# A two-layer attention trunk in split float32: side work moved off the key copies, gate products between transposes, value products in one batch, a merge ordered by branch

## The chip, the core and the metric

The kernel runs on one core of a Trainium2 chip. The engines are named as in the profile: PE is TensorE (matrix products), PEld its weight loads, DVE is VectorE, ACT is ScalarE, POOL is GpSimd and SP is SyncE, which issues the weight DMAs. The metric is the device time of one execution in microseconds (us); smaller is better.

## What is computed

A trunk of two layers over 256 context tokens and 256 latent tokens of width 1024. Cut to what matters here:

```python
for l in range(2):
    shift, scale, gate, shift2, scale2, gate2 = split(silu(c) @ w_ada[l] + b_ada[l])  # adaLN
    h = modulate(rms_norm(x), shift, scale)
    p = h @ w_in[l]                          # gate logits | c_q | c_kv | k_rope | na q,k,v
    mq = rms_norm(c_q) @ w_uq;  mk, mv = rms_norm(c_kv) @ w_ukv
    y_mla = softmax(norm(mq) @ norm(mk).T) @ mv              # 8 heads, all keys
    y_na = softmax([window scores + bias, context scores]) @ nv   # 8 heads
    g = sigmoid(gate logits)
    x = x + gate * ((g_a * (y_mla @ w_mla_o) + g_b * (y_na @ w_na_o)) @ w_out)
    x = x + gate2 * (relu(modulate(rms_norm(x), shift2, scale2) @ w_ff1) ** 2 @ w_ff2)
return x_latent
```

Context tokens attend to context tokens alone. In the second layer only latent tokens go on behind the keys and values, so its query side is 256 tokens wide instead of 512.

## The kernel before

All is float32, and every product is made of three passes on PE over operands split into a high and a low part (`mm3`, lines 99 to 103: high by high, low by high, high by low). A weight block of 0.5 MB is loaded raw on SP's queue, ACT makes its high part (L129), DVE the low part (L130); three split blocks can be held, five raw ones. PSUM is split into banks A (two), B (three), C (two) and D (one). In the first layer a product streams 512 columns, in the second 256.

Order of the stages in a layer: projections of `c_q`, `c_kv` and rope keys; queries (`w_uq`) and keys and values (`w_ukv`, copied out of PSUM at L738 by DVE and L739 by ACT, statistics at L604 and L605); six of the 16 gate blocks (`gates`, 24 PE products a block); latent attention (MLA), neighbourhood projections (`chunk_na`, keys, queries, values, 192 products of 256 columns each, with head norms on POOL at L608, L179 and L978), neighbourhood attention (NA), the rest of the gates, the merge (lines 1031 to 1060), the output projection and the feed-forward part. The tile scheduler writes the order of each engine from priorities: what `high_priority` marks goes first when ready, and products of later stages are put where nothing else was ready.

In an attention stage heads go in pairs. `prep_mla` and `prep_na` transpose queries and keys on PE into a bank C (lines 781, 786, 800, 805) and split them; scores go to banks B; `soft` makes the probabilities; `flip` transposes them (L872) and ACT (L876) and DVE (L878) copy them out; `mix` makes the value products (L892), in one batch for the context queries (four instructions) and one for the latent queries (eight).

The adaLN vectors of later use are side work on DVE: `ada_side`, with a product of a weight row by a scalar (L250), sums of further rows (L254), a transpose and a reduction (L265, L266) and a small PE product (L272). It is a generator, which `step(n)` advances by n parts; `step` is called once for every second key copy, once behind each block of `proj_a`, four times at the end of a feed-forward block, and `step(99)` ends it before a stage needs it. The lines of the key copy that the change touches:

```python
                if hf == 1 and tk % 2:
                    k_stat(tk - 1)
                if tk % 2:
                    step()
```

The merge, for each of eight column blocks j, makes the product of branch a (`ym`) and of branch b, then scales both by the gates (L1048), adds them (L1052) and splits the sum (L1053, L1054); the low part of the latent attention's output, `y1l`, is made by DVE at L1018 ahead of it.

Of the kernel before, what the change touches and what calls it, by code (L numbers as in the profile page):

```python
# [45 lines left out]
def trunk(ctx: ExitStack, tc, t):  # L46
# [77 lines left out]
    split = []  # L124

# [338 lines left out]
    for l in range(DEPTH):  # L464
# [218 lines left out]
        def gates(n, bank="A"):  # L683
            for _ in range(n):
                f = ngate[0]
                proj_a(w_in, 0, KD, f, 1, (H, Lo), c_q, lambda _, o: gate_evac(f, o), bank)
                ngate[0] += 1

# [43 lines left out]
        for hf in range(2):  # L732
            def evac(tk, o):
                hs = slice(hf * 4, (hf + 1) * 4)
                src = o.rearrange("p (h d) -> p h d", h=4)
                rs = rk[:, tk:tk + 1]
                dst = mk[:, tk, hs, 0:NOPE]
                nc.vector.tensor_copy(dst, src[:, :, 0:NOPE])  # L738
                nc.scalar.activation(out=mv[:, tk, hs, :], in_=src[:, :, NOPE:128], func=AF.Copy, scale=rs)  # L739
                head_ss(krr[:, tk, hs], dst, 4, NOPE, rs)  # L740
                if hf == 1 and tk % 2:
                    k_stat(tk - 1)
                if tk % 2:
                    step()
# [16 lines left out]
        gates(NG0[l], "B")  # L761
# [16 lines left out]
        def prep_mla(h):  # L778
            o = ps("C")
            for tk in range(q0, 4):  # L780
                nc.tensor.transpose(o[:QK, tk * 128:(tk + 1) * 128], mq[:, tk, h, :], ident)
# [3 lines left out]
            for tk in range(4):  # L785
                nc.tensor.transpose(o[:QK, tk * 128:(tk + 1) * 128], mk[:, tk, h, :], ident)
# [9 lines left out]
        def prep_na(hp):  # L796
            cs = slice(2 * hp * HD, (2 * hp + 2) * HD)
            o = ps("C")
            for tk in range(q0, 4):
                nc.tensor.transpose(o[:, tk * 128:(tk + 1) * 128], nqk[:, tk, cs], rev if tk >= 2 else ident)  # L800
# [3 lines left out]
            for tk in range(4):  # L804
                nc.tensor.transpose(o[:, tk * 128:(tk + 1) * 128], nqk[:, 4 + tk, cs], ident)
# [60 lines left out]
        def flip(P, K, perm):  # L866
            out = []
            for kp in range(K // 256):
# [5 lines left out]
                pT_ = ap.tile([128, 2, 256], F32, tag="PT", name="PT", bufs=4)  # L874
# [9 lines left out]
        def mix(yo, st, K, vsel, hp, ta, tb):  # L884

            oc = slice(st * 256, (st + 1) * 256)
            nkt = K // 128
            for kt in reversed(range(nkt)):
                for z, tr in ((1, tb), (0, ta)):
                    lead = z == 1 and kt == nkt - 1  # L890
                    with nullcontext() if lead else tc.high_priority(2000):
                        mm = nc.tensor.matmul(  # L892
                            yo[z * 64:(z + 1) * 64, oc], vsel(kt, 2 * hp + z), tr[kt // 2][:, kt % 2, :],
                            start=kt == nkt - 1, stop=kt == 0, tile_position=(0, z * 64))
                    if not lead:
                        tc.keep_in_program_order(mm)

        def attend_mla(vsel, ev):
            nxt = prep_mla(0)
            for hp in range(NH // 2):  # L900
                pa = nxt
                pb = prep_mla(2 * hp + 1)
                yo = ps("D")
                for gi, (toks, K, st) in enumerate(groups):
# [4 lines left out]
                    mix(yo, st, K, vsel, hp, ta, tb)  # L909
                ev(hp, yo[:, c_q])  # L910

        def attend_na(vsel, ev):

            nxt = prep_na(0)
            for hp in range(NH // 2):
# [13 lines left out]

                for gi, (toks, K, st) in enumerate(groups):  # L930
# [18 lines left out]
                    mix(yo, st, K, vsel, hp, ta, tb)  # L949
# [57 lines left out]
        gates(16 - ngate[0])  # L1007
# [24 lines left out]
        for f in range(0, 8, 2):  # L1032
# [4 lines left out]
            for j in range(2):  # L1037
                zs = [None, None]
                fs = slice(j * 128, (j + 1) * 128)
                g2 = g2f[:, :, j]  # L1040
                for b in (0, 1):
                    (h, lo), (yh, yl) = wab[b], ys[b]
# [3 lines left out]
                    zs[b] = o  # L1046
                for b in range(2):
                    nc.vector.scalar_tensor_tensor(out=g2[:, b], in0=g2[:, b], scalar=1.0, in1=zs[b],  # L1048
                                                   op0=ALU.add, op1=ALU.mult)
                eng = nc.vector if f + j >= 6 else nc.gpsimd  # L1050
                m = sp.tile([128, TT], F32, tag="tmp", name="m", bufs=NTMP)
                eng.tensor_tensor(out=m[:, :TQ], in0=g2[:, 0], in1=g2[:, 1], op=ALU.add)  # L1052
# [133 lines left out]
        def ff2(g, a):  # L1186
# [13 lines left out]
            step(4)  # L1200
# [53 lines left out]
        step(99)  # L1254
        pre_ctx = po_ctx
# [55 lines left out]
```

## Time and profile before

| | us |
|---|---|
| runs | 1308.4, 1308.9, 1310.21 |
| median | 1308.9 |
| profiled execution | 1308.73 |
| its span in the profile | 1306.9 |
| PE busy in the span | 1272.0 |
| DVE busy | 907.8 |
| ACT busy | 582.3 |
| POOL busy | 262.3 |

The span runs from the first to the last recorded instruction; the execution's own time is 1.8 us longer. In the first layer, by the trace: key projection to 125, gates to 157.6, MLA from its first score at 163.9 to its last value product at 237.3, neighbourhood projections to 282.3, NA to 352.2, the rest of the gates to 379.2. The hand-over to the second layer lies at 834 to 846, the second layer's merge at 1062 to 1077. A row of a timeline gives start, duration, engine, line, operation, output and inputs with their shapes, and in brackets the idle time in front with the instruction that ended it. PE's products overlap, so what a product costs is read from one start to the next, not from its duration.

### The profile page before, as it was taken

What the parts mean: (1) busy time and instruction counts of PE and PEld (TensorE: products, weight loads), DVE (VectorE), ACT (ScalarE), POOL (GpSimd) and SP (SyncE); (2) the same over time, 40 slices, a digit from 0 to 9 for tenths busy, and PEclk for the clock granted to TensorE, in tenths of its full rate; (3) what the DMA queues carried; (4) which work ended last, traced back from release to release, by engine and by line L of the source; (5) the groups of instructions that cost most, each with busy time, mean ns of one, the idle gap of its engine ahead of it and who ended that gap; (6) DMA issues with size and microseconds to landing.
All of it is one profiled execution on the core that took longest, in us unless ns stands there. A gap on an engine that the chain in (4) does not pass through costs nothing.

```text
span 1306.9 us, 20364 instructions
## 1 busy us (share of the span) xinstructions
PE 1272.0 (97%) x7831; PEld 1093.3 (84%) x7831; DVE 907.8 (69%) x1547; ACT 582.3 (45%) x1054; POOL 262.3 (20%) x258
## 2 busy tenths in 40 slices
PE   7998999999999999999999999899999999999997
PEld 5697888986787898888888888899889779999896
DVE  4559687688985579899675675766763967665553
ACT  4455277445523344422322312366664645554452
POOL 0317402411004003210201200019132111121011
PEclk9998999999999999999999999899999999999999
DMA  9855600364486326566566574387214657646652
GB/s 292 291 110 161 209 29 22 100 193 64 110 308 202 99 64 197 163 204 200 167 197 209 170 226 141 115 172 213 74 44 119 129 179 206 169 160 192 193 186 89
DMA packets 241857, 208.01 MB, mean 159 GB/s; under 512 B 24464, under 2 KB 220816, under 8 KB 241376
## 3 DMA queue, kind: packets, MB, share of 16 engines
q1 hardware_dynamic: 231728, 190.16, 50.6%
q10 hardware_dynamic: 9520, 16.29, 3.5%
q8 instruction: 61, 1.00, 0.3%
q0 software_dynamic: 512, 0.27, 0.1%
q14 instruction: 36, 0.29, 0.1%
HBM read 195.15 MB, written 11.53 MB: 158 GB/s over the span
## 4 chain that ended last, share of the span: by engine, by line
PE 55%; DVE 2%; POOL 2%; issue 2%; ACT 1%; DMA 0%; POOLq 0%; ACTq 0%; DVEq 0%
PE psB L101 7%; PE psB L103 7%; PE psB L102 7%; PE psA L101 6%; PE psA L103 6%; PE psA L102 6%; PE psC L103 4%; PE psC L101 4%; PE psC L102 4%; DVE wlo L130 1%; PE psC L872 1%; PE psD L892 1%; ACT whi L129 1%; PE psB L926 1%; PE psD L101 0%
## 5 line engine op out<-in xcount | busy, mean ns | idle before, releaser
L130 DVE TENSOR_TENSOR wlo<-raw,whi 128x1024 fp32r<-128x1024 f32 (+3 forms) x252 | 310.6, 1234 | 189.8 <-ACT whi L129 188.6
L129 ACT ACTIVATE whi<-raw 128x1024 fp32r<-128x1024 f32 (+3 forms) x252 | 260.5, 1035 | 351.3 <-PE psB L102 116.7
L254 DVE SCALAR_TENSOR_TENSOR ada<-raw,silu,ada 128x1024 f32<-128x1024 f32 (+1 forms) x126 | 156.3, 1272 | 0.2
L102 PE MATMUL psA<-wlo,h 128*128 128x256 f32 (+2 forms) x408 | 120.9, 296 | 2.4 <-DVE wlo L130 2.4
L101 PE MATMUL psA<-whi,h 128*128 128x256 f32 (+2 forms) x408 | 121.0, 297 | 1.1 <-ACT h L344 1.1
L103 PE MATMUL psA<-whi,h 128*128 128x256 f32 (+2 forms) x408 | 120.8, 296 | 0.0
L101 PE MATMUL psB<-h,whi 128*128 128x256 f32 (+1 forms) x272 | 91.8, 338 | 0.1
L102 PE MATMUL psB<-h,whi 128*128 128x256 f32 (+1 forms) x272 | 91.8, 338 | 0.0
L103 PE MATMUL psB<-h,wlo 128*128 128x256 f32 (+1 forms) x272 | 91.6, 337 | 0.0
L101 PE MATMUL psA<-h,whi 128*128 128x512 f32 (+1 forms) x248 | 87.6, 354 | 1.1 <-ACT h L344 1.0
L102 PE MATMUL psA<-h,whi 128*128 128x512 f32 (+1 forms) x248 | 87.3, 352 | 0.2 <-DVE h L346 0.2
L103 PE MATMUL psA<-h,wlo 128*128 128x512 f32 (+1 forms) x248 | 87.1, 351 | 0.0
L102 PEld LDWEIGHTS psA<-wlo,h 128*128 128x128 f32 x408 | 78.3, 192 | 4.7 <-DVE wlo L130 2.6
L101 PEld LDWEIGHTS psA<-whi,h 128*128 128x128 f32 x408 | 78.3, 192 | 3.3 <-ACT h L344 1.6
L103 PEld LDWEIGHTS psA<-whi,h 128*128 128x128 f32 x408 | 78.3, 192 | 2.3 <-issue 0.4
L1165 POOL TENSOR_TENSOR h<-s,h 128x512 fp32r<-128x512 f32 (+1 forms) x32 | 38.0, 1190 | 168.5 <-ACT h L1164 151.1
L1165 POOL TENSOR_TENSOR fl<-s,fa 128x512 fp32r<-128x512 f32 (+1 forms) x32 | 35.3, 1104 | 164.8 <-ACT fa L1164 164.8
L101 PE MATMUL psB<-G,whi 128*128 128x512 f32 (+2 forms) x192 | 66.8, 348 | 0.0
L103 PE MATMUL psB<-G,wlo 128*128 128x512 f32 (+2 forms) x192 | 66.3, 345 | 0.3 <-DVE wlo L130 0.3
L102 PE MATMUL psB<-G,whi 128*128 128x512 f32 (+2 forms) x192 | 66.5, 346 | 0.0
L101 PE MATMUL psC<-G,whi 128*128 128x258 f32 (+2 forms) x200 | 62.6, 313 | 0.0
L103 PE MATMUL psC<-G,wlo 128*128 128x258 f32 (+2 forms) x200 | 62.5, 312 | 0.0
(388 smaller groups left out, 3333.0 us busy)
## 6 DMA issues: line engine op xcount, KB each, us to landing
raw<-in_w_ff_dram SPq DMA_DIRECT2D x128, 512.0 KB, 4.3
raw<-in_w_ada_dram SPq DMA_DIRECT2D x80, 512.0 KB, 3.7
raw<-in_w_in_dram SPq DMA_DIRECT2D x62, 512.0 KB, 4.6
raw<-in_w_out_dram SPq DMA_DIRECT2D x16, 512.0 KB, 4.6
spare<-in_w_ada_dram SPq DMA_DIRECT2D x12, 512.0 KB, 8.9
xT_d<-xT SPq DMA_DIRECT2D x2, 2048.0 KB, 13.1
bias<-in_rpb_dram SPq DMA_DIRECT2D x64, 64.0 KB, 7.1
g_d<-g ACTq DMA_DIRECT2D x16, 256.0 KB, 3.9
```

Of the source, the lines that this page charges most:

```text
L101: nc.tensor.matmul(out, sh, mh, start=first, stop=False)
L102: nc.tensor.matmul(out, sh, ml, start=False, stop=False)
L103: nc.tensor.matmul(out, sl, mh, start=False, stop=last)
L129: nc.scalar.activation(out=hi, in_=src, func=AF.Copy)
L130: split[:] = [nc.vector.tensor_tensor(out=lo, in0=src, in1=hi.bitcast(F32), op=ALU.subtract).ins]
L254: nc.vector.scalar_tensor_tensor(out=a, in0=raw[:, c:c + w], scalar=sc, in1=a, op0=ALU.mult, op1=ALU.add)
L872: nc.tensor.transpose(o[:, kt * 256 + i * 128:kt * 256 + (i + 1) * 128], pt[:, (kp * 2 + kt) * 128:(kp * 2 + kt + 1) * 128], perm if K == ...
L892: mm = nc.tensor.matmul(yo[z * 64:(z + 1) * 64, oc], vsel(kt, 2 * hp + z), tr[kt // 2][:, kt % 2, :], start=kt == nkt - 1, stop=kt == 0, t ...
L926: mm = nc.tensor.matmul(os[z], q_[zs, cs], k_[zs, :K], start=n == 0, stop=n == 2)
L1165: nc.gpsimd.tensor_tensor(out=al[:, f, :], in0=s[:, :TQ], in1=ah[:, f, :].bitcast(F32), op=ALU.subtract)
```

## The change

Five edits. (1) The key copies no longer call `step`. (2) `pace`: behind the first `ff2` block of the first layer each block of `proj_a` calls `step(2)`, until the layer ends; the `step(4)` per `ff2` block is gone. (3) The gate blocks become a generator that yields one PE product at a time; in the first layer `chain` puts one of them, in fixed order, behind each transpose of queries and keys. In the second layer `chain` only raises the priority of the transposes behind the first. (4) `mix` takes both query groups of a pair, so their value products form one batch, the latent group first; the flipped probabilities of the context group get two tiles of their own (`PTc`). In the second layer there is one group, and its batch is as before. (5) The merge goes by branches: a for both column blocks of a pair, then b for both, each product scaled right away.

```diff
+    pace = [1]
...
                 evac(f + j, o)
                 flush()
-                step()
+                step(pace[0])
...
+        def gate_mms(bank):
+            while ngate[0] < 16:
                 f = ngate[0]
-                proj_a(w_in, 0, KD, f, 1, (H, Lo), c_q, lambda _, o: gate_evac(f, o), bank)
                 ngate[0] += 1
+                h, lo = wsplit(wraw(w_in, 0, KD, f * 128, 128), KD, 128)
+                o = ps(bank[0])[:, :TQ]
+                for k in range(KD):
+                    for n, (a, b) in enumerate(((h, H), (h, Lo), (lo, H))):
+                        yield nc.tensor.matmul(o, a[:, k], b(k)[:, c_q], start=k == n == 0, stop=k == KD - 1 and n == 2)
+                gate_evac(f, o)
+                flush()
+                step(pace[0])
+                yield None
...
+        def chain(trs):
+            for i, tr in enumerate(trs):
+                with nullcontext() if i == 0 else tc.high_priority(2000):
+                    mm = tr()
+                if l:
+                    continue
+                if i:
+                    tc.keep_in_program_order(mm)
+                with tc.high_priority(2000):
+                    g = next(gstream, None)
+                    if g is None:
+                        g = next(gstream, None)
+                if g is not None:
+                    tc.keep_in_program_order(g)
...
-                if tk % 2:
-                    step()
...
-            for tk in range(4):
-                nc.tensor.transpose(o[:QK, tk * 128:(tk + 1) * 128], mk[:, tk, h, :], ident)
+            chain([lambda tk=tk: nc.tensor.transpose(o[:QK, tk * 128:(tk + 1) * 128], mk[:, tk, h, :], ident)
+                   for tk in range(4)])
...
-                    mix(yo, st, K, vsel, hp, ta, tb)
+                    parts.append((st, K, ta, tb))
+                mix(yo, vsel, hp, parts)
...
-            for j in range(2):
-                zs = [None, None]
...
+            for b in (0, 1):
+                (h, lo), (yh, yl) = wab[b], ys[b]
+                for j in range(2):
...
-            step(4)
+            pace[0] = 2
```

DVE at the first key copies, before; `mqk` is the tile of queries and keys, `qrs` and `krr` the statistics, `ada` the side work:

```order
L130 TENSOR_TENSOR wlo<-raw,whi 128x1024
L254 SCALAR_TENSOR_TENSOR ada<-raw,silu,ada 128x512 x6
L605 TENSOR_REDUCE qrs<-sq 128x2
L254 SCALAR_TENSOR_TENSOR ada<-raw,silu,ada 128x512 x2
L605 TENSOR_REDUCE qrs<-sq 128x2
L130 TENSOR_TENSOR wlo<-raw,whi 128x1024
L738 COPY mqk<-psB 128x4x64 x2
```

and with the change:

```order
L131 TENSOR_TENSOR wlo<-raw,whi 128x1024
L606 TENSOR_REDUCE qrs<-sq 128x2
L131 TENSOR_TENSOR wlo<-raw,whi 128x1024
L606 TENSOR_REDUCE qrs<-sq 128x2
L774 COPY mqk<-psB 128x4x64 x2
L251 TENSOR_SCALAR ada<-raw,silu 128x512 x2
L606 TENSOR_REDUCE krr<-sq 128x4
L251 TENSOR_SCALAR ada<-raw,silu 128x512
```

All of the side work that stood ahead of the copies (two groups are shown) stands behind the first of them now, from its first product of a row and a scalar on.

PE at the end of a pair of the MLA stage (the third), before; the operands are `qk` for scores, `P` probabilities, `whi,h` a neighbourhood projection product, and `mv` values:

```order
L872 MATMUL psC<-ident,P 128x128 x4
L103 MATMUL psA<-whi,h 128x256
L872 MATMUL psC<-ident,P 128x128 x4
L102 MATMUL psB<-qk 128x256
L781 MATMUL psC<-ident,mqk 96x128 x4
L103 MATMUL psB<-qk 128x256
L102 MATMUL psB<-qk 128x256
L103 MATMUL psB<-qk 128x256
L892 MATMUL psD<-PT,mv 64x256 x8
L786 MATMUL psC<-ident,mqk 96x128 x4
L101 MATMUL psA<-whi,h 128x256
```

and with the change, at the end of the first pair (here `h,whi` is a gate product):

```order
L693 MATMUL psA<-h,whi 128x512
L815 MATMUL psC<-ident,mqk 96x128
L693 MATMUL psA<-h,wlo 128x512
L815 MATMUL psC<-ident,mqk 96x128
L693 MATMUL psA<-h,whi 128x512
L932 MATMUL psD<-PT,mv 64x256 x8
L932 MATMUL psD<-PTc,mv 64x256 x4
L820 MATMUL psC<-ident,mqk 96x128
L693 MATMUL psA<-h,whi 128x512
L820 MATMUL psC<-ident,mqk 96x128
```

The neighbourhood projection's products have left this place, each transpose of queries or keys is followed by a gate product, and the value products of both groups stand together. In the whole stage, from the first score to the last value product, 193 projection products become 48, and 48 gate products are added (16 more stand in front of it). Behind the stage 343 projection products become 528.

PE at the end of the neighbourhood projections, before, with the first pair's transposes behind the last value projection (`nqk` is the tile of queries and keys, `whi_3115` a block of the value projection):

```order
L102 MATMUL psA_3170<-wlo_3116,h_207 128x256
L103 MATMUL psA_3170<-whi_3115,h_208 128x256
L800 MATMUL psC_3231<-ident_70,nqk_2446 128x128 x2
L800 MATMUL psC_3231<-rev_72,nqk_2446 128x128 x2
L805 MATMUL psC_3240<-ident_70,nqk_2446 128x128 x4
L101 MATMUL psA_3977<-h_207,whi_3973 128x512
L102 MATMUL psA_3977<-h_208,whi_3973 128x512
```

and with the change, some 180 products earlier (`whi_3078` and `whi_3084` are the value projection's first blocks):

```order
L103 MATMUL psA_3088<-whi_3078,h_208 128x256
L834 MATMUL psC_3322<-rev_72,nqk_2537 128x128
L693 MATMUL psA_2263<-h_207,whi_2259 128x512
L101 MATMUL psA_3088<-whi_3084,h_207 128x256
L834 MATMUL psC_3322<-rev_72,nqk_2537 128x128
L693 MATMUL psA_2263<-h_208,whi_2259 128x512
L693 MATMUL psA_2263<-h_207,wlo_2260 128x512
L839 MATMUL psC_3335<-ident_70,nqk_2537 128x128
L693 MATMUL psA_2263<-h_207,whi_2259 128x512
```

The first two query transposes (L834) stand directly behind the query projection now, 12 products of the value projection come between them and the other two, of which the first row shows the last, 179 come later, and gate products stand between. Of the gates 81 products are left behind the last value product of NA instead of 118, and ahead of the second L272 product and of `y1l` PE has six merge products instead of 17.

## Rows read from the trace of the kernel before

**Rows 1.** Page, busy time of the engines over the span (us, share, instructions)

```profile
PE 1272.0 (97%) x7831; PEld 1093.3 (84%) x7831; DVE 907.8 (69%) x1547; ACT 582.3 (45%) x1054; POOL 262.3 (20%) x258
```

**Rows 2.** Table of windows: busy us (records) of each engine, granted clock, DMA

```profile
117.00:125.00 8.00, 7.23 (x22) 5.72 (x23) 8.00 (x16) 5.84 (x13) 7.68 (x9) 0.65 0.42 124
125.00:157.60 32.60, 32.60 (x145) 27.00 (x144) 25.56 (x32) 10.45 (x16) 21.69 (x19) 1.00 0.72 218
...
163.90:237.30 73.40, 72.36 (x535) 60.59 (x533) 57.53 (x163) 49.84 (x117) 12.79 (x12) 1.00 0.10 30
237.30:282.30 45.00, 45.00 (x367) 44.24 (x365) 29.88 (x33) 19.20 (x36) 14.96 (x12) 1.00 0.55 161
282.30:352.20 69.90, 68.95 (x425) 46.93 (x424) 62.62 (x151) 40.79 (x99) 6.38 (x5) 1.00 0.42 82
352.20:379.20 27.00, 27.00 (x121) 22.30 (x120) 25.25 (x24) 6.86 (x10) 0.00 (x0) 1.00 0.82 264
...
834.00:846.00 12.00, 7.95 (x41) 7.20 (x40) 9.27 (x25) 2.38 (x6) 0.70 (x1) 0.73 0.54 160
1062.00:1077.00 15.00, 12.69 (x98) 11.84 (x98) 7.24 (x15) 4.44 (x8) 5.10 (x6) 1.00 0.73 226
```

**Rows 3.** Timeline of PE at the first keys: start, us, line, [idle <-releaser]

```profile
112.45 0.39 PE L103 MATMUL psB<-whi,G 128*128 128x512 f32 x1
117.77 0.79 PE L101 MATMUL psB<-whi,G 128*128 128x512 f32 x1 [4.93 <-ACT mv L739]
```

**Rows 4.** Timeline of VectorE ahead of the key copies

```profile
108.91 4.06 DVE L254 SCALAR_TENSOR_TENSOR ada<-raw,silu,ada 128x512 f32<-128x512 f32 x6
...
113.15 2.26 DVE L254 SCALAR_TENSOR_TENSOR ada<-raw,silu,ada 128x512 f32<-128x512 f32 x2
```

**Rows 5.** Timeline of ScalarE, copy of the first values

```profile
117.24 0.47 ACT L739 ACTIVATE mv<-psB,rk 128x256 f32<-128x256 f32 x1 [7.47 <-DVE mqk L738]
```

**Rows 6.** Timeline of PE, last vector product and single and grouped transposes

```profile
160.96 0.33 PE L272 MATMUL psC<-red,m 128*128 128x64 f32 x2
161.12 0.60 PE L781 MATMUL psC<-ident,mqk 128*96 128x128 f32 x4
...
161.68 0.28 PE L103 MATMUL psA<-whi,h 128*128 128x256 f32 x1
...
202.76 0.28 PE L103 MATMUL psA<-whi,h 128*128 128x256 f32 x1
202.89 0.27 PE L872 MATMUL psC<-ident,P 128*128 128x128 f32 x1
...
203.11 0.28 PE L102 MATMUL psA<-wlo,h 128*128 128x256 f32 x1
```

**Rows 7.** Groups of PE by shape in 163.9 to 237.3 us (busy, mean ns)

```profile
L102 PE MATMUL psA<-wlo,h 128*128 128x256 f32 x65 | 19.0, 292 | 0.0
```

**Rows 8.** Timeline of ScalarE, last copy of the neighbourhood queries

```profile
255.72 0.66 ACT L973 ACTIVATE nqk<-psA 128x256 f32<-128x256 f32 x2 [0.38 <-PE psA L103]
```

**Rows 9.** Timeline of GpSimd, norm of the last query tokens

```profile
264.29 0.20 POOL L608 TENSOR_SCALAR nrs<-nrs 128x8 f32<-128x8 f32 x1
...
266.28 1.04 POOL L978 TENSOR_TENSOR nqk<-nqk,nrs 128x512 f32<-128x512 f32 x1
```

**Rows 10.** Timeline of VectorE from the last probabilities to the merge

```profile
346.50 0.48 DVE L842 TENSOR_SCALAR P<-P,ri 128x512 f32<-128x512 f32 x1
...
365.05 9.65 DVE L254 SCALAR_TENSOR_TENSOR ada<-raw,silu,ada 128x1024 f32<-128x1024 f32 x8
...
383.43 0.68 DVE L1018 TENSOR_TENSOR y1l<-yv,ym 128x512 fp32r<-128x512 f32 x1
```

**Rows 11.** Timeline of PE between the layers

```profile
836.92 0.40 PE L102 MATMUL psA<-wlo,h 128*128 128x288 f32 x1 [2.37 <-DVE wlo L130]
...
839.74 1.23 PE L330 MATMUL psC<-ident,rt 128*128 128x128 f32 x4 [0.56 <-POOL rt L179]
842.07 0.61 PE L101 MATMUL psA<-whi,h 128*128 128x288 f32 x1 [1.11 <-ACT h L344]
```

More of the change, by code (lines that the diff above doesn't have):

```diff
@@ L681, in trunk, with gates @@
         ngate = [0]
-        def gates(n, bank="A"):
-            for _ in range(n):
+        def gate_mms(bank):
+            while ngate[0] < 16:
                 f = ngate[0]
-                proj_a(w_in, 0, KD, f, 1, (H, Lo), c_q, lambda _, o: gate_evac(f, o), bank)
                 ngate[0] += 1
+                h, lo = wsplit(wraw(w_in, 0, KD, f * 128, 128), KD, 128)
[7 more added lines that the diff above has]
+                yield None
+        gbank = ["B"]
+        gstream = gate_mms(gbank)
+        def gates(n):
+            while n and ngate[0] <= 16:
+                mm = next(gstream, 0)
+                if mm == 0:
+                    return
+                n -= mm is None
+        def chain(trs):
[12 more added lines that the diff above has]
+                    tc.keep_in_program_order(g)
         if l == 0:
@@ L759, in trunk @@
             q_end = q_fin(tk)
-        gates(NG0[l], "B")
+        gates(NG0[l])
+        gbank[0] = "A"
         step(99)
@@ L779, in prep_mla @@
             o = ps("C")
-            for tk in range(q0, 4):
-                nc.tensor.transpose(o[:QK, tk * 128:(tk + 1) * 128], mq[:, tk, h, :], ident)
+            chain([lambda tk=tk: nc.tensor.transpose(o[:QK, tk * 128:(tk + 1) * 128], mq[:, tk, h, :], ident)
+                   for tk in range(q0, 4)])
             qh, ql = qk_tile(TQ), qk_tile(TQ)
@@ L798, in prep_na @@
             o = ps("C")
-            for tk in range(q0, 4):
-                nc.tensor.transpose(o[:, tk * 128:(tk + 1) * 128], nqk[:, tk, cs], rev if tk >= 2 else ident)
+            chain([lambda tk=tk: nc.tensor.transpose(o[:, tk * 128:(tk + 1) * 128], nqk[:, tk, cs],
+                                                     rev if tk >= 2 else ident) for tk in range(q0, 4)])
             qh, ql = qk_tile(TQ), qk_tile(TQ)
@@ L803, in prep_na @@
             o = ps("C")
-            for tk in range(4):
-                nc.tensor.transpose(o[:, tk * 128:(tk + 1) * 128], nqk[:, 4 + tk, cs], ident)
+            chain([lambda tk=tk: nc.tensor.transpose(o[:, tk * 128:(tk + 1) * 128], nqk[:, 4 + tk, cs], ident)
+                   for tk in range(4)])
             kh, kl = qk_tile(), qk_tile()
@@ L882, in trunk, with mix @@
         groups = ([] if last else [([0, 1], LC, 0)]) + [([2, 3], TT, 1)]
[L884 to L896, printed above, removed]
+        def mix(yo, vsel, hp, parts):
+            lead = True
+            for st, K, ta, tb in reversed(parts):
+                oc = slice(st * 256, (st + 1) * 256)
+                nkt = K // 128
+                for kt in reversed(range(nkt)):
+                    for z, tr in ((1, tb), (0, ta)):
+                        with nullcontext() if lead else tc.high_priority(2000):
+                            mm = nc.tensor.matmul(
+                                yo[z * 64:(z + 1) * 64, oc], vsel(kt, 2 * hp + z), tr[kt // 2][:, kt % 2, :],
+                                start=kt == nkt - 1, stop=kt == 0, tile_position=(0, z * 64))
+                        if not lead:
+                            tc.keep_in_program_order(mm)
+                        lead = False
         def attend_mla(vsel, ev):
@@ L948, in attend_na @@
                     ta, tb = (flip(p, K, rev) for p in P)
[L949 removed]
+                    parts.append((st, K, ta, tb))
+                mix(yo, vsel, hp, parts)
                 ev(hp, yo[:, c_q])
@@ L1005, in trunk @@
         attend_na(lambda kt, h: nv[:, kt, h * HD:(h + 1) * HD], ev_y2)
-        gates(16 - ngate[0])
+        gates(16)
         step(99)
@@ L1254, in trunk @@
         step(99)
+        pace[0] = 1
         pre_ctx = po_ctx
```

21 lines of the change are left out of this document (12 added, 9 removed).

## Prediction

> **What bounds the kernel now.** I read the page first. PE is busy 97% of the span, VectorE 69% and ScalarE 45% [rows 1], so time can be won at PE's few waits and clock dips, or by giving PE fewer products; and it is lost wherever PE's queue, which takes its instructions in order, meets a result that is not there. Next came the table of windows by stage [rows 2]. In the four attention stages of the first layer, 163.9 to 379.2 us, PE stands idle for about two microseconds in all. That is no proof that PE sets the length there: products that nothing waits for (the neighbourhood projection in the first stage, the gates later) are put into its gaps. In 163.9 to 237.3 us there are 193 such projection products (three lines, 65 of one of them in [rows 7]). At 0.12 us each, the slot that [rows 6] shows for one, they are 23 of PE's 72 us there. What is left, 49 us, is less than VectorE's 57.5 [rows 2]. So the stage is a chain through PE, ScalarE and VectorE, whose gaps are filled. The question for this change is where it takes the filling from.
>
> **Sum against the profiled execution**, 1308.7 us (span 1306.9), within 0.2 us of the median 1308.9.
>
> *Keys: -7.3.* The second bank of key products waits 4.93 us for a ScalarE copy [rows 3], which itself sat behind VectorE's first copy for 7.47 us [rows 5]. Ahead of that VectorE copy stand eight adaLN sums, six of which take 4.06 us [rows 4]. The change moves all of them behind the copies, so the wait goes whole, 4.9 to 5.1 us. After the wait the clock is 0.65 over the window 117 to 125: 22 products take 7.2 us, where the next window has 32.6 us for 145, or 0.225 each [rows 2]; 22 of those are 4.9 us, so 2.3 come back too. Nothing hides this gain, since PE is full behind it.
>
> *From the gates to the first score: +3.2.* The adaLN sums have not gone; 16 more of VectorE's short ones now lie between the key copies and the adaLN product in front of the first transposes, at 4.06/6 = 0.68 us each 10.8 us. Before, PE reached that product at 160.96 [rows 6] after filling its wait with 28 projection products (3.4 us); in the new order no product stands there. With no idle VectorE would be done just as PE is done with the gates (wait 0); with as much idle as before, 13 us late. I take 4, nearer to the lower end, since the gap that is seen there is 3.4. Gates 32.6, wait 4, and 16 transposes each with its gate product: a transpose costs 0.11 whether four stand together (161.12 to 161.68, less one product of 0.12) or one stands between products (202.76 to 203.11 less two products) [rows 6]. So 16 x 0.336 = 5.4, together 42.1 against 38.9 (125.0 to 163.9).
>
> *Transposes apart: 0.* By the same rows nothing is won by parting them: 0.11 each way. The Trainium skill's page "TensorE: Matmul & The Clock Gate", in its part on what happens when a matmul is issued, says that the next weights can be loaded during the running matmul, and gives 0.056 us from start to start at 128 columns; by that, a transpose behind a long product would cost half, and the 96 parted ones of this layer would give an estimated 5 us of PE time. The trace does not agree: 0.11 in both settings.
>
> *Latent attention, 73.4 us: 0.* In the new order 48 projection products are left there, 145 fewer (-17.4 us of PE work), with 48 gate products added (0.225 each, +10.8) and value batches joined (four fewer entries and exits at 0.2, -0.8). PE's work falls to about 65 us. Bounds: -8.7, if the stage is as short as that work; +7, if two of a pair's four groups of transposes lie on the chain, since four now take 1.35 us instead of 0.44. I take the length as it was, because the projection products that filled it held up nothing that a chain waits for.
>
> *Projection behind it, 45.0 us: +21.3.* The 145 products, with the 40 that used to fill the wait for the adaLN product and the first transposes, stand here now: 343 become 528. 185 x 0.12 = 22.2, less four gate products 0.9. This stage is PE alone (45.00 of 45.00 busy, [rows 2]), so nothing hides it.
>
> *A new wait in it: +5.4.* The query transposes now come straight behind the query projection, with 12 products between the second and the third and 179 value products behind the last. Their norms are GpSimd's, 3.0 us for a token (264.29 to 267.32, [rows 9]), one after another for four tokens. Before, the last was done at 267.3 while the last query copy began at 255.72 [rows 8]; less some 2.5 us of work between, PE would wait 9.1. At 3.0 a token from the same start (two tokens in the middle were slower) it is 5.4. I take that one.
>
> *Neighbourhood attention, 69.9 us: -3.* 23 fewer gate products, -5.2, and joined batches, -0.8; its chain gets the same longer transpose groups. Ends -6.9 (VectorE's 62.6 of work plus a little) and 0.
>
> *From there to the merge: 0.* VectorE needs 36.9 us from the last probabilities (346.50) to the first latent sum of the merge (383.43), eight long adaLN sums alone 9.65 [rows 10], and the change leaves that work where it is. PE has 81 gate products behind the last value product instead of 118, and six merge products instead of 17: some 8 to 10 us of its 27 become a wait, and the length stays. Ends -8 and +2.3 (a clock dip as at the keys).
>
> *Second layer's start: -4.* Doubling the step during the last feed-forward lets the adaLN vectors end before the hand-over. The wait of 2.37 us for split weights goes; the one of 0.56 and that of 1.11 [rows 11] belong to the norm and may stay. The clock is 0.73 in that window, with PE busy for 8 us [rows 2]; a quarter of that, some 2 us, is the clock's, and I count 1.6 of it as the other waits stay. Ends -6 and +3, if denser steps hold up the weight splits that precede them on VectorE.
>
> *Merge by branches: 0.* In the first layer it is inside the wait above. In the second PE stands 2.3 us of 15 [rows 2], for splits of either branch in turn: -1.5 to +1.5.
>
> Sum: -7.3 + 3.2 + 21.3 + 5.4 - 3 - 4 = +15.6, **1324 us**.
>
> **Rivals.**
> *The stages shrink to their work.* Against the 0 at the latent attention: what leaves a queue lets the rest start earlier. Then that stage gives -8.7 and the neighbourhood one -6.9: 1308.7 - 7.3 + 3.2 - 8.7 + 21.3 + 5.4 - 6.9 - 4 = 1312, and 1306 if GpSimd's norms come in time too. For it: PE is full before. Against: VectorE, ScalarE and PE take turns on banks of which the transposes have two. It decides by a pair's length: 16.2 us instead of 18.4.
>
> *No new wait: faster.* If every gap that loses its filling closes (the adaLN product on time, pairs of latent attention below 15.5 us, GpSimd ahead, VectorE's rest moved into its idle time), PE's slots alone count: keys -7.3, joined batches -1.6, pace -4: 1296. For it are PE's 97%; against it VectorE's 57.5 in the latent stage and the fixed 36.9 us ahead of the merge. It turns to the other side once the new waits add up to under 13 us; I expect about 28.
>
> *The clock falls in the new waits.* At the keys one wait of 4.9 us was followed by products at 0.43 us in place of 0.225 and a clock of 0.65 [rows 2, 3], and the stretch between the layers, 66% busy, had 0.73. The latent stage would be 88% busy, in shorter gaps. With 0.73 there, 64.7 us of PE work become 88.6: 1339; with a dip only behind GpSimd's wait and ahead of the merge (2.3 each), 1329. The Trainium skill's page "TensorE: Matmul & The Clock Gate", section on HAM oscillation, has the same as a rule: gaps between bursts send the clock back to 1.2 GHz, and each burst starts there. The trace agrees at the keys; whether gaps this short do it, no run here shows.
>
> *The pace does nothing* (the vectors still end at the hand-over, held by their weight loads): +4, 1328, inside the forecast.
>
> **How the numbers follow.** The forecast, lengths kept and projection laid bare, 1314 to 1331: 0.61. Stages at their work, 1305 to 1314: 0.15, of which 0.02 faster, 0.06 same, 0.07 slower, with 0.2% (2.6 us) about what a measurement of this kernel can tell from no change. No new wait, 1290 to 1303: 0.12. Clock falling, 1331 to 1339: 0.12. So faster 0.14, same 0.06, slower 0.80. A range of 1302 to 1336 leaves out most of the third case and a part of the fourth, under 0.2.
>
> **What would show it.** Keys: no wait over 1 us at the first key products and a clock of 1.0 behind them. Latent attention: 72 to 76 us long with PE at about 65 busy; if the stage is 65 long, the first rival holds. The projection stage should take 70 to 75 us, with PE waiting for GpSimd at the third and fourth query transpose. Ahead of the merge PE should wait 8 to 10 us for VectorE's adaLN reduction or the latent sum. Between the layers no transpose and reduction of adaLN sums and no wait for split weights. The forecast is wrong if PE's busy share stays at 97%, or if the stretch from the first score (163.9) to the first latent sum of the merge (383.4) has not grown by 15 us or more from its 219.5.

## The result, and the profile after

The changed kernel takes 1359.8 us (median of 4 runs, 1353.7 to 1364.8) against 1309.6 for the kernel before: a ratio of 1.038, interval 1.034 to 1.043. It is slower, as forecast, but by 50 us where 15 were forecast, and outside the range. The profiled execution took 1353.7 us with a span of 1351.9, 45.0 more than before. The four runs of the changed kernel lie 11 us apart, the longer ones at a lower granted clock (mean 0.988 in the profiled one, the shortest, and 0.977 in the longest); stages below are read from the profiled one.

The page's first part after, to [rows 1]:

```profile
PE 1281.4 (95%) x7831; PEld 1093.8 (81%) x7831; DVE 916.7 (68%) x1547; ACT 584.0 (43%) x1054; POOL 265.8 (20%) x258
```

PE has the same 7831 products, yet it stands idle for 70 us instead of 35, and its busy time is 9 us up, in part where the clock was low (the windows of 0.69 to 0.98 below). The table of windows of the changed kernel, to [rows 2], by its own stages (us; busy us and records of PE, PEld, DVE, ACT, POOL; granted clock; DMA):

```profile
149.90:164.10 14.20, 7.48 (x36) 5.41 (x35) 9.88 (x18) 3.50 (x5) 0.00 (x0) 0.76 0.51 160
164.10:246.70 82.60, 70.39 (x433) 50.59 (x431) 51.21 (x154) 45.86 (x104) 0.00 (x0) 0.98 0.07 20
246.70:333.50 86.80, 72.28 (x546) 68.57 (x544) 38.59 (x43) 27.16 (x51) 27.21 (x24) 0.96 0.37 109
333.50:403.40 69.90, 64.09 (x401) 43.56 (x399) 61.54 (x146) 39.33 (x98) 6.55 (x5) 0.98 0.41 75
403.40:428.40 25.00, 20.63 (x93) 16.65 (x91) 24.84 (x31) 6.89 (x9) 0.00 (x0) 0.96 0.83 267
428.40:436.00 7.60, 7.60 (x24) 5.96 (x25) 6.20 (x12) 0.00 (x0) 0.00 (x0) 0.69 1.02 385
```

Stage by stage, from one landmark on PE to the next (first and last products of each, so that bounds differ from the table's by a few tenths):

| stage of the first layer | before | after | forecast | measured |
|---|---|---|---|---|
| to the start of the gates | 125.0 | 117.4 | -7.3 | -7.6 |
| gates to the first score | 38.9 | 46.7 | +3.2 | +7.8 |
| latent attention | 73.1 | 82.3 | 0 | +9.2 |
| to the first neighbourhood score | 45.3 | 87.1 | +26.7 | +41.9 |
| neighbourhood attention | 69.7 | 69.6 | -3 | -0.1 |
| to the adaLN product of the merge | 31.6 | 25.2 | 0 | -6.4 |
| merge | | | 0 | +2.6 |

That is +47.4 when the output projection starts. Later the last feed-forward's first part loses 2.0, the hand-over gains 5.8 (-3.8 together, forecast -4), the keys of the second layer lose 1.8, and its merge gains 1.2.

Timeline of PE of the changed kernel between the gates and the first scores:

```profile
149.82 0.39 PE L693 MATMUL psB<-h,wlo 128*128 128x512 f32 x1
156.92 0.69 PE L273 MATMUL psC<-red,m 128*128 128x64 f32 x2 [6.72 <-DVE red L267]
...
160.35 0.27 PE L820 MATMUL psC<-ident,mqk 128*96 128x128 f32 x1
160.38 0.48 PE L693 MATMUL psA<-h,wlo 128*128 128x512 f32 x1
160.70 0.27 PE L820 MATMUL psC<-ident,mqk 128*96 128x128 f32 x1
```

The adaLN product waits 6.72 us for VectorE, where [rows 6] had a wait filled with projection products. A transpose with its gate product takes 0.35 us (160.35 to 160.70); less 0.225 for the product, 0.12 is left for the transpose, as [rows 6] had it. Parting them saves nothing.

In latent attention itself (164 to 246.5 us) PE now waits 4.6 us in all for the split queries and keys that are made from the transposes; the kernel before has no such wait there:

```profile
PE psB L101 <- ACT qk L806: 2.5, 2, 1.3
PE psB L102 <- DVE qk L807: 1.6, 3, 0.7
PE psC L907 <- DVE qk L807: 0.5, 1, 0.5
```

Waits of PE in the stretch behind latent attention (246.4 to 333.6 us: what for, us in total, times, longest), and its timeline at the last query transpose and in the products behind it:

```profile
PE psC L834 <- POOL nqk L1023: 7.4, 3, 4.2
PE psA L101 <- ACT nqk L1018: 4.5, 6, 0.7
PE psA L102 <- DVE wlo L131: 2.6, 3, 0.9
```

```profile
307.65 0.47 PE L834 MATMUL psC<-rev,nqk 128*128 128x128 f32 x1 [4.21 <-POOL nqk L1023]
...
310.91 0.41 PE L103 MATMUL psA<-whi,h 128*128 128x256 f32 x1
311.12 0.41 PE L101 MATMUL psA<-whi,h 128*128 128x256 f32 x1
```

Three waits for GpSimd's norms were forecast. The second line was not: six times a projection product waits for ScalarE to copy the bank before it, which before never happened in this stage (45.00 busy of 45.00, [rows 2]). The open gate block sits in one of the two banks A, so the projection has one bank, and one of three split weight blocks is gone as well. Behind GpSimd's last wait products take 0.21 instead of 0.12 us.

Timeline of VectorE ahead of the merge, to [rows 10], and of PE at the merge:

```profile
397.64 0.45 DVE L877 TENSOR_SCALAR P<-P,ri 128x512 f32<-128x512 f32 x1
...
408.00 14.43 DVE L255 SCALAR_TENSOR_TENSOR ada<-raw,silu,ada 128x1024 f32<-128x1024 f32 x12
...
428.24 0.68 DVE L1063 TENSOR_TENSOR y1l<-yv,ym 128x512 fp32r<-128x512 f32 x1
```

```profile
428.38 0.69 PE L273 MATMUL psC<-red,m 128*128 128x64 f32 x2 [4.37 <-DVE red L267]
...
430.25 0.63 PE L101 MATMUL psB<-ym,whi 128*128 128x512 f32 x1
430.68 0.71 PE L102 MATMUL psB<-y1l,whi 128*128 128x512 f32 x1
```

From the last probabilities to the first latent sum VectorE needs 30.6 us instead of 36.9, with twelve of its 14 adaLN sums in one piece, fewer weight splits between them (three instead of six) and without two waits of its own (1.7 us for the high part of a weight, 1.7 us for a DMA). So PE waits 4.4 us instead of the 8 to 10 forecast, and the products behind that wait go at 0.43 us.

### The profile page after: what moved, and what is told of

It reads as the page before. It is cut to its first block, busy times and chain, and to the rows that moved or that the text cites. A ratio compares the mean times of both kernels' runs of the same rounds, so it can differ in the third digit from the quotient of the medians.

```text
span 1351.9 us, 20385 instructions
## 1 busy us (share of the span) xinstructions
PE 1281.4 (95%) x7831; PEld 1093.8 (81%) x7831; DVE 916.7 (68%) x1547; ACT 584.0 (43%) x1054; POOL 265.8 (20%) x258
## 4 chain that ended last, share of the span: by engine, by line
PE 50%; DVE 4%; DMA 2%; issue 2%; POOL 2%; ACT 1%; ACTq 0%; POOLq 0%; SPq 0%; DVEq 0%
PE psB L101 6%; PE psB L103 6%; PE psB L102 6%; PE psA L103 6%; PE psA L101 6%; PE psA L102 6%; PE psC L101 3%; PE psC L102 3%; PE psC L103 3%; DVE wlo L131 2%; ACT whi L130 1%; PE psD L932 1%; PE psC L907 1%; DMA raw<-in_w_na_o_dram 1%; PE psB L693 1%
## 5 line engine op out<-in xcount | busy, mean ns | idle before, releaser
L255 DVE SCALAR_TENSOR_TENSOR ada<-raw,silu,ada 128x1024 f32<-128x1024 f32 (+1 forms) x126 | 159.6, 1304 | 0.5
L693 PE MATMUL psA<-h,whi 128*128 128x512 f32 (+1 forms) x288 | 87.3, 380 | 0.0
L1209 POOL TENSOR_TENSOR fl<-s,fa 128x512 fp32r<-128x512 f32 (+1 forms) x32 | 35.1, 1097 | 165.5 <-ACT fa L1208 165.5
L101 PE MATMUL psC<-G,whi 128*128 128x258 f32 (+2 forms) x200 | 62.7, 314 | 0.0
L102 PE MATMUL psC<-G,whi 128*128 128x258 f32 (+2 forms) x200 | 62.5, 312 | 0.0
L693 PEld LDWEIGHTS psA<-h,whi 128*128 128x128 f32 x288 | 51.7, 196 | 10.5 <-issue 4.0
L102 PE MATMUL psB<-h,whi 128*128 128x512 f32 (+1 forms) x160 | 55.1, 345 | 0.0
L101 PE MATMUL psB<-h,whi 128*128 128x512 f32 (+1 forms) x160 | 54.9, 344 | 0.0
L103 PE MATMUL psB<-h,wlo 128*128 128x512 f32 (+1 forms) x160 | 54.9, 343 | 0.0
```

What stands on the lines that cost most here:

```text
L101: nc.tensor.matmul(out, sh, mh, start=first, stop=False)
L102: nc.tensor.matmul(out, sh, ml, start=False, stop=False)
L103: nc.tensor.matmul(out, sl, mh, start=False, stop=last)
L255: nc.vector.scalar_tensor_tensor(out=a, in0=raw[:, c:c + w], scalar=sc, in1=a, op0=ALU.mult, op1=ALU.add)
L693: yield nc.tensor.matmul(o, a[:, k], b(k)[:, c_q], start=k == n == 0, stop=k == KD - 1 and n == 2)
L1209: nc.gpsimd.tensor_tensor(out=al[:, f, :], in0=s[:, :TQ], in1=ah[:, f, :].bitcast(F32), op=ALU.subtract)
```

## The experiments

Theory A: the gate block that is interleaved does nearly all the damage. Theory B, at first its rival, is that the gate products lengthen latent attention's chain itself. Outright rivals were the joined batches and the moved side work. A product is called pinned here when it has a fixed place in PE's order, at raised priority; filling is what the scheduler puts where nothing else was ready. A slot is the time from one product's start to the next: 0.12 us for a projection product, 0.225 for a gate product. Where no interval is given there is one run, and it is read by its stages.

**1. No interleaving.** In `chain`, the gate products are left out; they go where the scheduler puts them.

```diff
-                if l:
-                    continue
+                continue
```

> The changed kernel, but transposes of queries and keys go without a gate product behind each; the gates stay a generator and all other edits stay. Theory A (the interleaved gate block does the damage: while it is open it holds one of the two banks A and one of three split weight blocks, so the neighbourhood projection finds no place in latent attention and later runs from one bank) and theory B (the gate products lengthen the chain of latent attention itself) both say that the 47 us lost in the first layer go: about 1297 to 1302 us, with keys 7.6 us earlier than in the kernel before, latent attention 72 to 75 us long, projections behind it 43 to 47. The rival, that the joined value batches or the side work moved behind the keys are what costs, says that it stays above 1335 us.

Measured: 1300.3 us, ratio 0.993 (0.991 to 0.995). Its table of windows, latent attention and the stretch behind it:

```profile
157.90:230.90 73.00, 70.33 (x519) 58.59 (x518) 57.21 (x163) 49.86 (x117) 12.96 (x12) 1.00 0.12 36
230.90:275.60 44.70, 44.70 (x365) 43.74 (x361) 29.86 (x33) 19.15 (x36) 14.96 (x12) 1.00 0.55 160
```

Both stages are as before, the 47 us are gone, and the other four edits together make the kernel faster than the kernel before. The outright rivals fall.

**2. Interleaving alone**, in the kernel before.

```diff
-            for tk in range(4):
-                nc.tensor.transpose(o[:QK, tk * 128:(tk + 1) * 128], mk[:, tk, h, :], ident)
+            chain([lambda tk=tk: nc.tensor.transpose(o[:QK, tk * 128:(tk + 1) * 128], mk[:, tk, h, :], ident)
+                   for tk in range(4)])
```

(the same at the three other groups, with the gate generator)

> The kernel before with the interleaved gates alone. If they are the whole loss: latent attention 80 to 84 us (73.1 before), from there to the first neighbourhood score 84 to 90 us (45.3 before), in all 1350 to 1365 us. If the loss needs the other edits too (joined batches, fewer side steps), under 1335 us.

Measured: 1365.3 us; latent attention 81.8, the stretch behind it 87.1. The loss needs no other edit.

**3. The gate block in a bank B.**

```diff
-        gbank[0] = "A"
```

> The changed kernel, but a gate block accumulates in one of the three banks B instead of one of the two banks A. Theory A: projections have both banks A again, so 158 of their products stand in latent attention instead of 48 and 418 instead of 528 behind it; without waits for the copy from the single bank the stretch behind it falls from 87 to about 68 us, and with it the time to 1335 to 1342 us; latent attention stays near 82 us if its length is the chain's (theory B, transposes with gate products between), and falls to 73 to 76 us if it was the missing bank.

Measured: 1369.5 us. The stretch behind latent attention falls to 67.4 as expected, but latent attention grows to 90.5:

```profile
165.50:256.00 90.50, 84.48 (x543) 65.03 (x541) 56.27 (x160) 50.04 (x114) 1.55 (x2) 0.96 0.10 30
256.00:323.40 67.40, 58.66 (x440) 55.64 (x436) 35.03 (x37) 22.64 (x41) 25.08 (x23) 0.90 0.44 124
```

The expected total and both expected lengths of latent attention were missed. With gates in fixed places, the bank decides how much of the projection goes into latent attention, and that is the part of theory A that holds. But the 110 products that return (13 us of slots) cost 8 us there, where 193 of them cost nothing before. The bank that the gates hold is now one of the three that the scores use, and this run does not tell what that costs from what the pinned place costs. The whole is worse also for a reason of the edit: the gates of the second layer stay in bank B too. Its neighbourhood attention is no longer than before (47.3 us from the first score to the last value product, 50.1 before), but 166 gate products, which had filled it, now come behind it, where four did: the stage starts 49.8 us later than before and the merge behind it 66.5 (60.8 at the end). There filling that had to share banks with the scores was left out of the stage, with nothing pinned.

**4. The open block ended** before the neighbourhood projections.

```diff
+        if l == 0:
+            gates(1)
         for part in (1, 0, 2):
```

> The changed kernel, but the open gate block is ended before the neighbourhood projections begin (one more whole block there), so that they have both banks A and the value projection comes ahead of the first transposes. Theory A: the waits for the copy (4.5 us) and for GpSimd's norms (7.4 us) go, with the low clock behind them (about 4 us): the stretch behind latent attention falls from 87 to 68 to 72 us, in all 1336 to 1342 us, and latent attention keeps its 82 us. If the stretch is long only for its 185 additional products and their weights, it stays above 80 us.

Measured: 1352.0 us. The stretch takes 69.5 us, as expected, with no wait for bank or norms:

```profile
167.70:255.70 88.00, 77.24 (x433) 56.22 (x431) 51.71 (x153) 46.10 (x102) 0.00 (x0) 0.88 0.09 28
255.70:325.20 69.50, 67.82 (x556) 66.56 (x552) 41.02 (x46) 28.40 (x56) 27.46 (x24) 1.00 0.51 145
```

That gives 17 us of this stretch to the open block. The time fell by less, because latent attention, with as many PE records as in the changed kernel (433, eight more of them gate products), took 88.0 us at a clock of 0.88 instead of 82.6 at 0.98, and neighbourhood attention 74.7 at 0.89. The expected total, 1336 to 1342 us, was missed.

**5. Gate products behind the group** of four transposes instead of between them; same stream, same order otherwise.

```diff
             for i, tr in enumerate(trs):
                 with nullcontext() if i == 0 else tc.high_priority(2000):
                     mm = tr()
-                if l:
-                    continue
-                if i:
+                if not l and i:
                     tc.keep_in_program_order(mm)
+            for _ in trs if not l else ():
                 with tc.high_priority(2000):
                     g = next(gstream, None)
```

> The changed kernel, but the four transposes of a group stand together and their four gate products behind them; what stands in which stage is nearly as in the changed kernel (45 projection products in latent attention, 531 behind it). If the gate products between the transposes lengthen the chain of latent attention (a group ends 0.9 us later), that stage falls from 82 us to 73 to 77 and the time by 5 to 10 us; if any gate product pinned there does it, because the copies of one group must wait for a queue of pinned work, the stage stays at 80 to 84 us. The stretch behind it stays at 85 to 90 us in both cases, since the open block is still there.

Measured: 1348.4 us.

```profile
165.00:239.30 74.30, 65.52 (x430) 49.61 (x428) 50.19 (x151) 43.93 (x99) 0.00 (x0) 1.00 0.08 22
239.30:327.10 87.80, 72.14 (x553) 68.31 (x549) 39.41 (x45) 28.28 (x55) 27.20 (x24) 0.96 0.38 107
```

Latent attention falls from 82.3 to 74.1, and no wait of PE in it names split queries or keys any more: the spacing of the transposes is worth 8.2 of its 9.2 us, some of it perhaps the clock's (0.98 there in the changed kernel, 1.00 here; 2% of the stage is 1.7 us). The stretch behind it stays.

**6. Keys alone** and **7. pace alone**, each in the kernel before.

```diff
-                if tk % 2:
-                    step()
```

> The kernel before without the side work at the key copies, in both layers. The 4.9 us wait and the low clock behind it go in the first layer (7.3 to 7.6 us by the changed kernel's trace); the adaLN product in front of the first transposes has its wait filled by projection products and costs nothing. 1300 to 1303 us. If the side work only moves and is paid for later in the first layer, 1307 to 1310 us.

Measured: 1304.5 us, between the two ranges. The 7.5 us are there at the start of the gates, and 5.1 are left at the first score: VectorE's sums now end later behind the gates, and 20 more projection products (48 instead of 28, 2.4 us) fill PE's wait for them there. By the end 4.2 of the span are left.

```diff
-                step()
+                step(pace[0])
...
-            step(4)
+            pace[0] = 2
```

> The kernel before with the doubled step in the last feed-forward of the first layer alone. The hand-over gives 5 to 6 us and the feed-forward loses 1.5 to 2 us to late weight splits, as in the changed kernel: 1304 to 1306 us. If the gain at the hand-over is taken back at the keys of the second layer (the weights come no earlier there), 1307 to 1310 us.

Measured: 1307.1 us, span 1.6 under that of before, as the second expectation had it. The hand-over gains about 6, the feed-forward loses 2.0 and the second layer's keys 1.7: its waits of PE from 640 to 900 us name a weight split (1.0) and the copy of the first values (1.3) in place of the 2.4 for a weight split of [rows 11]:

```profile
PE psA L101 <- ACT mv L740: 1.3, 1, 1.3
PE psA L103 <- DVE wlo L131: 1.0, 1, 1.0
```

**8. Keys, pace and merge** without the interleaved gates and the joined batches: the two edits above with the merge by branches.

```diff
+            zs = {}
+            for b in (0, 1):
+                (h, lo), (yh, yl) = wab[b], ys[b]
+                for j in range(2):
```

> The kernel before with the key edit, the pace and the merge by branches, without the interleaved gates and the joined value batches. If the three add up: -7.5 at the keys, -4 net of the feed-forward at the hand-over, -1 at the second merge, +2 to +4 at the keys of the second layer (weights later than the work): 1297 to 1301 us. If the joined batches carried part of the gain of the kernel without interleaving (1300.3), 1301 to 1305 us.

Measured: 1301.3 us, ratio 0.994 (0.992 to 0.995), at the border of the two ranges: it does not decide on the joined batches.

**9. Spacing, bank and block together** (the edits of experiments 3, 4 and 5).

> The changed kernel with the three edits together: gate products behind the group of transposes, gate block in a bank B, block ended before the neighbourhood projections. 96 projection products stand in latent attention, 480 behind it. If the causes found so far (spacing, bank, norms of GpSimd) are the whole loss: latent attention 75 to 79 us, the stretch behind it 480 x 0.12 + 5 = 62 to 65, in all 1325 to 1332 us; what is left over the kernel before is then the wait for the adaLN product and projection products that no longer stand in latent attention. If adding fillers lengthens latent attention again (as with bank B alone, 90 us), over 1340 us.

Measured: 1343.8 us, so the expected total was missed. In front of the second layer's neighbourhood attention it is 25.0 us behind the kernel before (the changed kernel 45.4); when the merge behind that stage starts, 39.8, with 166 gate products behind the stage again as in experiment 3, and 35.1 at the end. The first layer by windows, and the stretch in the second:

```profile
163.50:246.10 82.60, 76.85 (x489) 58.99 (x487) 56.16 (x157) 49.56 (x111) 0.00 (x0) 0.98 0.08 23
246.10:308.80 62.70, 61.09 (x502) 59.92 (x498) 38.38 (x42) 23.88 (x46) 27.45 (x24) 1.00 0.57 168
1020.00:1062.00 42.00, 35.59 (x221) 26.82 (x222) 25.13 (x51) 17.48 (x38) 3.40 (x3) 0.84 0.42 73
```

Latent attention is 8 us longer than in experiment 5 for 51 more projection and 8 more gate products, 7.9 us of slots. That is as if, with gates in fixed places, every further product added its own length; but the scores have a bank less here, too, and the clock was 0.98 instead of 1.00, so the cause of these 8 us is not shown.

**10. Keys, pace and joined batches** (merge as before), and **12.** the same with the side work kept at the second layer's keys (`if l and tk % 2: step()`).

> The kernel before with the key edit, the pace and the joined value batches; no interleaved gates, merge as before. By the sum of what was seen: 1301.3 less 1.6 for eight batches fewer, less 0.8 for the first layer's merge in its old order: 1298 to 1300 us. If the merge by branches was worth having, 1301 to 1303 us.

> As the kernel with key edit, pace and joined batches, but the side work stays at the key copies of the second layer. If its removal there costs 0.6 us at the second layer's keys, 0.5 to 1 us faster than that kernel; if that loss is a late weight load behind a shorter hand-over, the same within 0.5 us.

Measured: 1299.7 us, ratio 0.9925 (0.991 to 0.994), and 1300.1, ratio 0.992 (0.991 to 0.994). They can't be told apart, nor from experiment 1; all three lie 9 to 10 us under the kernel before.

**11. Merge by branches alone.**

> The kernel before with the merge by branches alone. If the trace of the kernel with keys, pace and merge is read rightly, the first layer's merge takes 0.8 us longer and the second's gains 0 to 1: 1308 to 1311 us, the same within what can be told. If it saves the 1.5 us wait for a weight split in each layer, 1305 to 1307 us.

Measured: 1307.9 us, span 0.8 under that of before: the same within what can be told. In the first layer the wait of 1.5 us for a weight split becomes two of 1.0, for both parts of a split.

**13. The same stream of gate products, not pinned**: behind each group, without fixed order or raised priority, in bank A.

```diff
-                with tc.high_priority(2000):
-                    g = next(gstream, None)
-                    if g is None:
-                        g = next(gstream, None)
-                if g is not None:
-                    tc.keep_in_program_order(g)
+            for _ in trs if not l else ():
+                if next(gstream, None) is None:
+                    next(gstream, None)
```

> The changed kernel with the same stream of gate products offered behind each group of transposes, in the same bank A, but without the fixed order and the raised priority: the scheduler may put them, like any other product, where nothing else is ready. In its order 144 projection products and 32 gate products stand in latent attention (48 and 48 in the changed kernel), 432 and 4 behind it. If the fixed place is what takes the filling out of the gaps, latent attention takes 72 to 76 us with both kinds in it, the stretch behind it 432 x 0.12 plus 5 to 8 for GpSimd's norms plus some 7 for the single bank, 64 to 68 us, and all 1318 to 1330 us. If projection products lengthen latent attention whenever gate blocks stand in it (as with bank B, 90 us), that stage is over 80 us and all 1338 us or more.

Measured: 1314.4 us.

```profile
161.10:233.30 72.20, 72.18 (x521) 59.94 (x519) 55.11 (x161) 48.52 (x113) 1.15 (x2) 1.00 0.14 43
233.30:302.10 68.80, 57.87 (x446) 55.71 (x444) 34.33 (x37) 22.53 (x41) 26.55 (x23) 0.95 0.41 119
```

Latent attention holds 144 projection and 32 gate products in 72.2 us, with PE busy throughout: the same bank and stream as in the changed kernel, and 10 us less.

The run to set beside it is experiment 5, where the gate products stand behind the group as well, but pinned: 45 projection products in 74.3 us, with 8.7 us of waits. So the pinned place (its fixed order and its raised priority, which were taken away together) is what took the filling out of the gaps; the single bank alone does not, since PE has no gap left in this stage. Unpinned, 20 more gate products also stand in front of the first score, and the time from the gates to that score is 41.9 us instead of 47.9. The whole lies under the expected 1318 to 1330 us. The stretch behind stays 23 us longer than before (89 more projection products, 10.7 us, GpSimd's norms 7.8, the single bank 2.2, a clock of 0.95).

From the changed kernel's 1359.8 us, then, the spacing takes off some 11 (experiment 5), the pinned place 34 (1348.4 to 1314.4) and what is left of the interleaving, with the block still open, 14 (to experiment 1's 1300.3). Two of these four times are single runs, and the changed kernel's own runs lie 11 us apart, so the first and the last step are rough.

## Why the prediction was wrong

**Right** were the direction and five terms: the keys (-7.3; measured -7.6, wait gone and clock 1.00 behind it), the price of a transpose (0.11 apart as together; 0.12 measured), the 185 displaced projection products (+21.3 by slots), GpSimd's norms (+5.4; 7.4), and the pace (-4; -3.8, of which the second layer's keys took 1.8 back). Early weight loads, of which the Trainium skill's page "TensorE: Matmul & The Clock Gate" speaks in its part on what happens when a matmul is issued, do stand in the trace: the weights of the transpose at 160.70 are loaded from 160.49 on for 0.13 us, while the gate product of 160.38 runs. The transpose still costs 0.12 us, and the 5 us that the prediction estimated from that page's figure are not there. Two slips in the prediction's sums (42.1 for 42.0 us up to the first score, 64.7 for 65.0 us of PE work in latent attention) change nothing.

**Wrong** in its mechanism was the step "Latent attention, 73.4 us: 0" (measured +9.2). It took the chain's length as given, on the ground that filling is put only into gaps, and set the longer transpose groups against the lost filling. But the gate products are not filling: they are pinned behind transposes and stand on the chain. Experiment 5 gives 8.2 us to the spacing, a little over the bound of +7 that the text named for two groups of a pair on the chain: that bound was the value to take, not the middle. Experiment 13 shows the other side: unpinned and behind the group, the stage is 72.2 us with more in it.

The second step that failed, and the larger miss, is "Projection behind it" with its "A new wait in it": 26.7 forecast, 41.9 measured. The products were counted rightly and priced at 0.12, the slot of a projection that alternates between two banks. The open gate block took one of them: 4.5 us of waits for the copy and 2.6 for split weights. GpSimd's wait was 2.0 longer than taken, and the low clock behind it (0.21 instead of 0.12 a product) was put into a rival and not into the sum. Experiment 4, with the block ended, brings the stretch to 69.5. That the block was left open for the whole stage stood in the order that was read, and the sum gave it no term.

The term "From the gates to the first score" was +3.2 and came to +7.8: the wait for VectorE was 6.7 where 4 was taken, and its sums were priced at 0.68 us, where thirteen of those beside the gates took 12.3 us, 0.95 each; and the first four pairs of a transpose and a product behind it ran at the low clock (0.64 us each, 157.40 to 159.97, instead of 0.35). "From there to the merge: 0" rested on VectorE's 36.9 us being fixed; they were 30.6. That is a mistake to the good, -6.4, which the merge's products at the low clock took back in part (+2.6).

Of the rivals, the one that let the stages shrink to their work didn't happen in the changed kernel. The clock that falls in the new waits did happen, behind three of them (windows of 0.76, 0.69 and 0.96), and hardly in latent attention in the profiled run (0.98); in experiment 4 nearly the same products ran there at 0.88. What sets the clock apart between such runs stays open. The sign by which the forecast was to be known as wrong did not appear: from the first score to the first latent sum of the merge the time grew from 219.5 to 264.1 us and PE's share fell to 95%. It guarded against too small a loss alone; the lengths named beside it, 72 to 76 us for latent attention and 70 to 75 for the projections, were the signs that failed (82.3 and 87.1).

## What to carry to other kernels

A product that fills a gap and one that is pinned to a place are not the same load: the first costs nothing while there is a gap, the second lies on the chain that it is pinned to, and takes the gap's work away with it. Before a piece of work is left half done for a long time, ask what it holds (a bank, a weight buffer) and who else needs that in the meantime. And when five edits come together, time them apart: here four of them were worth 9 us together, and the fifth cost 60.

## What the runs showed of the hardware

Transposes that stand singly behind a 512-column product cost 0.12 us each, against 0.11 in a group, although the load of their weights falls into the product in front (0.13 us from 160.49, the product from 160.38). The clock fell to its lower level in waits of 6.7, 4.4 and 4.2 us, and products behind them took 0.43 instead of 0.225 us and 0.21 instead of 0.12. VectorE's short adaLN sums took 0.68 us each where GpSimd was idle (five in 3.39 us, from 146.30) and 0.95 where it was at work beside them (seven in 6.66 us, from 138.16). That GpSimd is at work does not decide it alone: it was busy for 3.9 of the 4.06 us in which six sums took 0.68 each in [rows 4], and for 2.2 of the 2.26 us in which two took 1.13 each.
